# Four edits to a hybrid attention / state-space trunk step: a rotary table loaded earlier, softmax denominators of two heads inverted together, sample loads taken in turn, and a longer modelled pause

## The chip, the cores and the metric

The kernel runs on one core of one Trainium2 chip. The metric is the device time of one execution in microseconds (us). The engines are called as the profile calls them: PE (TensorE), DVE (VectorE), ACT (ScalarE), POOL (GpSimd), SP (SyncE, which here only issues DMAs). L383 is line 383 of the kernel.

## The reference

Two layers of a trunk in which three head groups work side by side on the same normalised input: latent attention, a matrix memory (mLSTM) and a gated delta rule. A layer, cut to what the change touches:

```python
proj = rms_norm(x, norm_w) @ w_in          # c_q, c_kv, k_r, z_a, ... z_m, z_g
q = (rms_norm(c_q, q_norm) @ w_uq).reshape(B, L, 8, 64 + 32)
q_nope, q_rope = q[..., :64], apply_rope(q[..., 64:], pos)
c_new = rms_norm(c_kv, kv_norm)            # latent of 256
o_a = mla_attention(q_nope, q_rope, c_all, kr_all, w_uk, w_uv, ...)
...
mixed = concat([o_a * silu(z_a), o_m * silu(z_m), o_g * silu(z_g)])
return x + mixed @ w_out, c_new, kr_new, ...
```

One new stream of 1024 frames and 16 meta tokens (the prompt) and 8 running streams of 16 frames (the samples) are stepped together: 1168 columns in all. The prompt's attention builds keys and values per head, with a chunk-causal mask. A sample attends, in latent space, over 1040 cached latents and its own 16 frames, so 8 batches of cache are read from HBM in each layer.

## The kernel before

Activations lie with features on the 128 rows (partitions) and the 1168 columns along the free side, in three slices (400, 384 and 384 columns). Wide tiles are "pages": a pool of 28, taken by `pg()` and given back by `free`; `room(n)` says whether n are free, `need(n)` waits for that. A value in float32 is multiplied as a high and a low part: `split` (L436 to L441) casts the high part on ACT and subtracts for the low part on DVE or POOL in turn, and `mm3` makes three matmuls of them.

The program is written by a weaver. Threads (`prep`, `att`, `samp_load`, `samp_ln`, ...) are Python generators; what one yields is a modelled number of microseconds to pause, or the name of an event to wait for. In the pauses the weaver writes the next piece of a filler: the projections, then `qkv` (queries, keys and values of the prompt), then the output projection. So the modelled pauses set the order in which instructions stand. On the chip each engine takes its own in that order, and waits on semaphores. `ld` (L382) issues loads on SP, whose loads and stores all stand in one queue; SP waits at the head of the queue for a buffer to come free.

**rstd** (L476) makes the column `1/sqrt(mean square)` and spreads it over 128 rows. PE sums squares with `onesb`, DVE scales (L495), POOL takes the power (L496), DVE splits it (L499, L500) and writes it into diagonal matrices (L506, L508). After a pause of 2.70 PE multiplies those by `onesr`. With `b16` it sums from a bfloat16 pair; that form is called six times in a layer, from `prep`, for the latent and the query part.

**prep** (L1343) normalises and splits the latents ckv (2 tiles) and cq (3 tiles), with two new pages for each tile. **qkv** waits until it is done and 10 pages are free, takes two for the rotary tables `tabq` and loads them, and computes query tiles; the first reads cq alone, the next reads the tables at L1420 and L1423.

**att** (L1568) runs over 8 heads, and for a head over three column pieces (336, 384 and 320 wide). The value matrix carries a block of ones, so the accumulator `po` holds the numerators on 64 rows and the denominators on the other 64; even and odd heads have them the other way round. The finish of a piece is five lines, L1612 to L1617: reciprocal of 64 rows on DVE, product of `po` and the gate z on DVE, product with the reciprocal on POOL, store from the ACT queue. z was loaded by SP into the tile "Og" (2 buffers) when the piece began, 64 rows at a time.

**The samples.** `samp_prep` (L1627) makes latent queries; `samp_load` (L1667) takes, for each batch, two pages of transposed latents (latT) and one of rotary keys (krT); `samp_ln` (L1709) takes latents in natural order (latN) with their last 32 rows from `latE` and `tok`; `samp_split` splits; `samp_s` computes scores and exponentials (L1753); `samp_t` transposes the weights and multiplies them by latN. Their first batches are woven into the last heads of `att`.

Of the kernel before, what the change touches and what calls it, by code (L numbers as in the profile page):

```python
# [19 lines left out]
T = 1168  # L20
# [287 lines left out]
def _build(nc, tc, ctx, I, O, layers):  # L308
# [29 lines left out]
    def room(n):  # L338
        return len(pages) + n <= NPG
# [136 lines left out]
    def rstd(out, a, dim, s0, s1, b16=False):  # L476
        w = s1 - s0
        tl = [c for c in range(NT) if s0 <= OFF[c] < s1]
        ps = pb()
        col = wt("col", 8)  # L480
        V.memset(col, 1.0)
        if b16:
            ab = wt("th", 800, 2, BF16)
            ah, al = ab[:, :w], ab[:, 400:400 + w]
            S.copy(ah, a)
            V.tensor_sub(al, a, ah)
        for j, c in enumerate(tl):
            n, o = LEN[c], OFF[c] - s0
            if b16:
                mm(ps[:n, j:j + 1], ah[:, o:o + n], onesb, True, False)  # L490
                mm(ps[:n, j:j + 1], al[:, o:o + n], onesb, False, True)
            else:
                mm(ps[:n, j:j + 1], a[:, o:o + n], ones[:, 0:1], True, True)
        for j0, j1, n in (((0, 1, 16), (1, len(tl), 128)) if tl[0] == 0 else ((0, len(tl), 128),)):
            V.tensor_scalar(col[:n, j0:j1], ps[:n, j0:j1], 1.0 / dim, EPS, op0=ALU.mult, op1=ALU.add)  # L495
        G.tensor_tensor(col[:, 0:len(tl)], col[:, 0:len(tl)], negh(len(tl)), op=ALU.pow)  # L496
        nt = len(tl)
        ch = wt("ch", 8, 2, F32R)
        V.tensor_copy(ch[:, 0:nt], col[:, 0:nt])  # L499
        V.tensor_sub(col[:, 0:nt], col[:, 0:nt], ch[:, 0:nt].bitcast(F32))  # L500
        dg = wt("dg", 1024, 1, F32R)
        first = 16 if tl[0] == 0 else 0
        for e, c_ in enumerate((ch, col)):
            o = 512 * e
            if first:
                V.tensor_scalar_mul(dg[:, o:o + 16], ident[:, 0:16], c_.bitcast(F32)[:, 0:1])  # L506
            m = nt - (first > 0)
            V.tensor_tensor(dg[:, o + first:o + w].rearrange("p (j t) -> p j t", t=128),  # L508
                            ident.unsqueeze(1).to_broadcast([128, m, 128]),
                            c_.bitcast(F32)[:, nt - m:nt].unsqueeze(2).to_broadcast([128, m, 128]), op=ALU.mult)  # L510
        yield 2.70
        ps = pb()
        for e in range(2):
            mm(ps[:, :w], onesr, dg[:, 512 * e:512 * e + w], e == 0, e == 1)
        if out is None:
            return ps[:, :w]
        S.copy(out, ps[:, :w])
# [69 lines left out]
    def layer(l, XH, XLp, XL, xres, xw, R):  # L587
# [755 lines left out]
        def prep():  # L1343
            yield ("cq", 2)
            yield from need(2)
            cq = [D1["cq", j] for j in range(3)]
            ckv = [D1["ckv", j] for j in range(2)]
            r1, r2 = pg(), pg()
            for s0, s1 in SLICES:
                w = s1 - s0  # L1350
                yield from rstd(r1[:, s0:s1], sumsq(ckv, w, s0, s1), 256.0, s0, s1, True)
                yield from rstd(r2[:, s0:s1], sumsq(cq, w, s0, s1), 384.0, s0, s1, True)
            while not room(4):
                yield 3.47
            yield 5.44
            hl = {}
            for n_, p_, r_, v_ in (("ck", ckv, r1, "kvn"), ("cq", cq, r2, "qn")):
                hl[n_] = []
                for k, t_ in enumerate(p_):
                    yield from need(2)  # L1360
                    hi, lo = pg(F32R), pg(F32R)
                    for s0, s1 in SLICES:
                        norm_split(t_, r_[:, s0:s1], vcol(l, v_, k), hi, lo, s0, s1)
                        yield 6.23
                    hl[n_].append((hi, lo))
                    if n_ == "cq":
                        free(t_)
                free(r_)
                if n_ == "ck":
                    for k in range(2):  # L1370
                        st(O["oLat"][l, k], ckv[k][:, :T])
                        G.tensor_copy(new[:, 128 * k:128 * k + 128], ckv[k][:, TP:T])
                    ps = pb()
                    for k in range(2):
                        tr(ps[:, 128 * k:128 * k + 128], ckv[k][:, TP:T], ident)
                    t_ = wt("hp", 528, 3)
                    S.copy(t_[:, 0:256], ps[:, 0:256])
                    st(tokS, t_[:, 0:256])
                    free(*ckv)
                A.update({n_ + "h": [x_[0] for x_ in hl[n_]], n_ + "l": [x_[1] for x_ in hl[n_]]})  # L1380
            D1["prep"] = 1

        KS = ((0, 348), (348, 694), (694, 1040))

        def qkv():
            while "prep" not in D1 or not room(10):
                yield "idle"
            tab, qs = [pg(), pg()], pg()
            A["qs"] = qs
            for j in range(2):  # L1390
                ld(tab[j][:, :T], I["tabq"][j])
            ckh, ckl, cqh, cql = A["ckh"], A["ckl"], A["cqh"], A["cql"]

            def load(t_):
# [172 lines left out]

        def att():  # L1568
            steps = [(h, s_, j) for h in range(8) for s_ in range(3) for j in range(9) if QB[j] < QS_[s_][1]]
            fly, po, zt = [], None, {}  # L1570
            for i_ in range(len(steps) + LA):
                if i_ < len(steps):
                    h, s_, j = steps[i_]
                    if s_ == j == 0:
                        while ("row", h) not in D1:
                            yield 0.3
                        yield max(0.0, D1["row", h] - W.t / 1000.0)
                    a, b = max(QS_[s_][0], QB[j]), QS_[s_][1]
                    if j == 0:
                        zt[h, s_] = z = wt("Og", 512)[64 * (h % 2):64 * (h % 2) + 64, :b - a]  # L1580
                        ld(z, mixS[8 + h // 2][64 * (h % 2):64 * (h % 2) + 64, a:b])
                    m = 80 if j == 0 else 128
                    qh, ql, kh, kl = A["sets"][h % 3]
                    ks = slice(KB[j], KB[j] + m)
                    ps = pb()[:m, :b - a]
                    mm(ps, kl[0:96, ks], qh[0:96, a:b], True, False)
                    mm(ps, kh[0:113, ks], qh[0:113, a:b], False, False)
                    mm(ps, kh[0:96, ks], ql[0:96, a:b], False, True)
                    pt = wt(("Tp", "M")[i_ % 2], 512)
                    S.activation(pt[:m, :b - a], ps, AF.Exp, scale=-1.0)  # L1590
                    fly.append((h, s_, j, a, b, m, pt))
                    if s_ == 2 and j == 8:
                        D1["hd", h] = 1
                        if h > 4:
                            free(*A["sets"][h % 3])
                if i_ >= LA:
                    h, s_, j, a, b, m, pt = fly.pop(0)
                    q0 = QS_[s_][0]
                    nj = sum(x_ < QS_[s_][1] for x_ in QB)
                    if j == 0:  # L1600
                        yield "v"
                        while A.get("fill", 0) and npa[0] - A["fill"] > 1:
                            yield 0.1
                        po = pa()
                        A["po"] = npa[0]
                    x_ = 4 * j + h // 2
                    v = VV_(x_ // 6)[:m, 192 * (x_ % 6) + 64 * (h % 2):192 * (x_ % 6) + 64 * (h % 2) + 128]
                    mm(po[:, a - q0:b - q0], v, pt[:m, :b - a], j == 0, j == nj - 1)
                    if j == nj - 1:
                        w = b - q0  # L1610
                        r, d = slice(64 * (h % 2), 64 * (h % 2) + 64), slice(64 - 64 * (h % 2), 128 - 64 * (h % 2))
                        rc, z = wt("hp", 528, 3)[r, :w], zt.pop((h, s_))  # L1612
                        V.reciprocal(rc, po[d, :w])  # L1613
                        V.tensor_mul(z, po[r, :w], z)
                        G.tensor_mul(z, rc, z)
                        A["po"] = 0
                        S.dma_start(mixS[8 + h // 2][r, q0:b], z)  # L1617
                yield YX
            free(*A["VV"])
            D1["att"] = 1  # L1620
# [46 lines left out]
        def samp_load():  # L1667
            yield "sprep"
            fly = A["fly"] = []
            for b in range(8):  # L1670
                for k in range(3):
                    while len(fly) >= RP or not room(1 + SR):
                        yield 0.30
                    raw = pg()
                    fly.append(raw)
# [316 lines left out]
```

## Time and profile before

| what | before |
| --- | --- |
| median of 3 runs | 2650.75 us (2647.45 to 2651.11) |
| the profiled execution | 2646.51 us, of which the span of the trace is 2644.6 |
| PE busy | 2488.7 us, 94% of the span |
| DVE, ACT, POOL busy | 58%, 42%, 29% |
| mean DMA rate | 98 GB/s |
| mean granted clock of PE | 0.978 of full |

The profiled execution lies a little under all three timed runs. PE is idle for some 156 us of the span; the rest of its time is work, apart from stretches in which the granted clock is half. "Waits" are idle time of an engine, put down to the instruction whose end released it.

### The profile page before, as it was taken

The page shows a single profiled execution, that of the slowest core. Times are in us where ns is not written, and L with a number is a line of the kernel's source. Part 1 is how long each engine was busy: PE and PEld are TensorE (multiplying, and loading weights), DVE is VectorE, ACT ScalarE, POOL GpSimd, SP SyncE. Part 2 cuts the span into 40 slices and gives each one's busy share as a digit, 9 for nine tenths or more (in the row PEclk, how much of TensorE's full clock was granted, in tenths as well). Part 3 has the DMA queues.
Part 4 walks back from the last instruction along what each step waited for, and adds up shares of the span by engine and source line. Part 5 has one row for each costly group of instructions (what it writes and reads, how often), then busy time and mean ns, then how long its engine had stood idle before and what let it go on. Part 6 is the DMA issues. An engine that isn't in the chain of part 4 may idle for free. (4 is left out here: it accounts for less than half of the span.)

```text
span 2644.6 us, 45521 instructions
## 1 busy us (share of the span) xinstructions
PE 2488.7 (94%) x17310; PEld 2150.1 (81%) x17310; DVE 1530.2 (58%) x3716; ACT 1116.4 (42%) x2635; POOL 764.6 (29%) x865
## 2 busy tenths in 40 slices
PE   6999999999999899979998999999999999999997
PEld 4887888878878789779977888788788788897896
DVE  6667475464453476654566774755743526665636
ACT  5363444444433433442343544444444434334612
POOL 3122222122123543232441222221221245332414
PEclk9999999999999999989998999999999999998998
DMA  3212112121123644464422121221211245444832
GB/s 130 73 39 70 51 53 83 51 69 51 59 71 126 179 119 123 126 219 163 141 76 51 43 75 52 62 73 51 69 52 58 85 157 149 113 121 147 286 117 80
DMA packets 158411, 258.67 MB, mean 98 GB/s; under 512 B 48704, under 2 KB 110768, under 8 KB 158192
## 3 DMA queue, kind: packets, MB, share of 16 engines
q1 hardware_dynamic: 152224, 247.59, 30.0%
q0 software_dynamic: 1856, 3.86, 0.7%
q10 hardware_dynamic: 4112, 4.30, 0.7%
q8 instruction: 137, 2.24, 0.3%
q14 instruction: 82, 0.67, 0.1%
HBM read 190.77 MB, written 64.92 MB: 97 GB/s over the span
## 5 line engine op out<-in xcount | busy, mean ns | idle before, releaser
L361 PE MATMUL pa<-pg,wh 128*128 128x384 f32 (+3 forms) x6324 | 1317.8, 351 | 17.7 <-DVE pg L441 7.0
L361 PEld LDWEIGHTS pa<-pg,wh 128*128 128x128 f32 x6324 | 1104.6, 190 | 59.9 <-issue 8.5
L361 PE MATMUL pb<-pg,pg 128*128 128x352 f32 (+26 forms) x1908 | 425.1, 338 | 18.3 <-DVE sm L1553 4.4
L361 PE MATMUL pa<-pg,wb 128*128 128x384 bf16 (+1 forms) x2208 | 420.3, 330 | 4.7 <-POOL pg L544 3.6
L361 PEld LDWEIGHTS pb<-pg,pg 128*128 128x128 f32 (+7 forms) x1908 | 301.1, 188 | 70.8 <-issue 14.0
L361 PEld LDWEIGHTS <-wb 128*128 128x128 bf16 x2208 | 201.6, 98 | 141.6 <-issue 28.9
L361 PE MATMUL pb<-wk,pg 128*128 128x128 f32 (+4 forms) x2168 | 223.1, 250 | 20.2 <-ACT wk L983 5.2
L441 POOL TENSOR_TENSOR wh<-wf,wh 128x1024 fp32r<-128x1024 f32 (+1 forms) x61 | 144.4, 2367 | 323.1 <-ACT wh L437 316.7
L361 PEld LDWEIGHTS pb<-wk,pg 128*128 128x128 f32 (+3 forms) x2168 | 194.2, 161 | 41.9 <-issue 16.7
L1590 ACT ACTIVATE wk<-pb 128x320 f32<-128x320 f32 (+8 forms) x288 | 114.1, 407 | 241.9 <-PE pb L361 222.5
L361 PE MATMUL pa<-wk,pg 128*128 128x320 f32 (+8 forms) x576 | 190.9, 417 | 1.9 <-ACT wk L1590 1.3
L437 ACT CAST wh<-wf 128x1024 fp32r<-128x1024 f32 (+1 forms) x122 | 126.4, 1036 | 129.8 <-PE pa L361 119.5
L1553 DVE TENSOR_REDUCE sm<-pb 128x1 f32<-128x348 f32 (+9 forms) x232 | 107.9, 493 | 102.4 <-PE pb L361 89.9
L1613 DVE RECIPROCAL wk<-pa 64x320 f32<-64x320 f32 (+2 forms) x48 | 110.7, 2305 | 48.2 <-PE pa L361 47.5
L361 PE MATMUL pb<-wk,wk 32*32 32x16 f32 (+6 forms) x1776 | 110.6, 216 | 13.7 <-DVE wk L1131 4.5
L1531 POOL TENSOR_TENSOR pg<-pg,pg 64x520 fp32r<-64x520 f32 (+1 forms) x64 | 86.9, 1369 | 111.0 <-ACT pg L1530 87.9
L868 DVE SCALAR_TENSOR_TENSOR pg<-pg,vec,pg 128x1192 f32<-128x1192 f32 x72 | 107.1, 1503 | 18.4 <-ACT pg L866 18.1
L441 DVE TENSOR_TENSOR wh<-wf,wh 128x1024 fp32r<-128x1024 f32 (+1 forms) x61 | 78.6, 1289 | 53.5 <-ACT wh L437 53.4
L693 ACT COPY pg<-pa 128x384 f32<-128x384 f32 (+1 forms) x108 | 52.1, 482 | 134.6 <-PE pa L361 133.4
L457 ACT CAST wb<-wf 128x1024 bf16<-128x1024 f32 x92 | 96.2, 1045 | 26.6 <-PE pa L361 20.1
L361 PEld LDWEIGHTS pa<-wk,pg 128*128 128x128 f32 (+1 forms) x576 | 97.9, 193 | 5.9 <-ACT wk L1590 1.9
L361 PEld LDWEIGHTS pb<-wk,wk 32*32 32x32 f32 (+2 forms) x1776 | 73.1, 122 | 32.3 <-issue 9.3
(298 smaller groups left out, 3205.7 us busy)
## 6 DMA issues: line engine op xcount, KB each, us to landing
wf<-win SPq DMA_DIRECT2D x92, 512.0 KB
pg<-latT SPq DMA_DIRECT2D x32, 520.0 KB
pg<-latN SPq DMA_DIRECT2D x32, 512.0 KB
wf<-wout SPq DMA_DIRECT2D x24, 512.0 KB
xa<-wk SPq DMA_DIRECT2D x40, 192.0 KB
mix<-pg SPq DMA_DIRECT2D x12, 584.0 KB
pg<-mix SPq DMA_DIRECT2D x12, 584.0 KB
mix<-pg SPq DMA_DIRECT2D x12, 576.0 KB
```

Source lines behind the costliest of these rows:

```text
L361: W.last = P.matmul(out, lhsT, rhs, start=start, stop=stop)
L437: S.copy(hi, src)
L441: lo_eng.tensor_sub(lo, src, hi.bitcast(F32))
L457: S.copy(wb[:, :n], wf)
L693: S.copy(o[:, s0:s1], ps)
L868: V.scalar_tensor_tensor(y[:, :n], cb[:, j:j + n], vcol(l, "cw", 4 * ti + j), y[:, :n], op0=ALU.mult, op1=ALU.add)
L1531: G.tensor_sub(lo, raw, hi.bitcast(F32))
L1553: V.tensor_reduce(mx[:LEN[c], 3 * c + i_:3 * c + i_ + 1], ps[:LEN[c], :n1 - x_], axis=AX.X, op=ALU.min)
L1590: S.activation(pt[:m, :b - a], ps, AF.Exp, scale=-1.0)
L1613: V.reciprocal(rc, po[d, :w])
```

## The change

1. `rstd` yields 4.00 instead of 2.70 for its `b16` calls.
2. `prep` takes the two table pages and loads them right after the latents' pages are freed, before cq is split; `qkv` waits for 8 free pages instead of 10.
3. `att` loads z once for a pair of heads, 128 rows, into tiles that alternate between the tags "Og" and "H". At each head's end ACT copies the denominators into their half of a 128-row tile, and DVE multiplies numerators by z. Only at the odd head one reciprocal runs over 128 rows, POOL multiplies, and one store of 128 rows follows: 24 loads, 24 reciprocals, 24 POOL products and 24 stores in each layer become 12 of each, and 24 copies on ACT are added.
4. `samp_load` loads batch b only after latN of batch b-1 has been issued.

```diff
-        yield 2.70
+        yield 4.00 if b16 else 2.70
...
                     free(*ckv)
+                    A["tab"] = [pg(), pg()]
+                    for j in range(2):
+                        ld(A["tab"][j][:, :T], I["tabq"][j])
...
         def qkv():
-            while "prep" not in D1 or not room(10):
+            while "prep" not in D1 or not room(8):
                 yield "idle"
-            tab, qs = [pg(), pg()], pg()
+            tab, qs = A["tab"], pg()
             A["qs"] = qs
-            for j in range(2):
-                ld(tab[j][:, :T], I["tabq"][j])
...
-                    if j == 0:
-                        zt[h, s_] = z = wt("Og", 512)[64 * (h % 2):64 * (h % 2) + 64, :b - a]
-                        ld(z, mixS[8 + h // 2][64 * (h % 2):64 * (h % 2) + 64, a:b])
+                    if j == 0 and h % 2 == 0:
+                        zt[s_] = z = wt(("Og", "H")[(3 * h // 2 + s_) % 2], (512, 516)[(3 * h // 2 + s_) % 2])[:, :b - a]
+                        ld(z, mixS[8 + h // 2][:, a:b])
...
-                        rc, z = wt("hp", 528, 3)[r, :w], zt.pop((h, s_))
-                        V.reciprocal(rc, po[d, :w])
-                        V.tensor_mul(z, po[r, :w], z)
-                        G.tensor_mul(z, rc, z)
+                        if h % 2 == 0:
+                            dt_[s_] = wt("hp", 528, 3)[:, :w]
+                        rc, z = dt_[s_], zt[s_]
+                        S.copy(rc[r], po[d, :w])
+                        V.tensor_mul(z[r], po[r, :w], z[r])
+                        if h % 2:
+                            V.reciprocal(rc, rc)
+                            G.tensor_mul(z, rc, z)
+                            S.dma_start(mixS[8 + h // 2][:, q0:b], z)
                         A["po"] = 0
-                        S.dma_start(mixS[8 + h // 2][r, q0:b], z)
...
-                    while len(fly) >= RP or not room(1 + SR):
+                    while len(fly) >= RP or not room(1 + SR) or b and ("ln", b - 1) not in D1:
                         yield 0.30
```

On ACT, before the first query tile of layer 0, the kernel before has these rows (L462 are the silus of the gate projections, L437 with `wh` a weight's high part, L1427 the end of the query tile's slices); the casts of cq stand further up, ahead of the silus shown:

```order
L462 ACTIVATE wk_8862<-pa_8833 128x400
L462 ACTIVATE wk_8892<-pa_8866 128x384
L437 CAST wh_9071<-wf_9070 128x768
L462 ACTIVATE wk_8925<-pa_8896 128x384
L1377 COPY wk_8956<-pb_8953 128x256
L462 ACTIVATE wk_8971<-pa_8930 128x400
L462 ACTIVATE wk_9001<-pa_8975 128x384
L462 ACTIVATE wk_9034<-pa_9005 128x384
L437 CAST wh_9076<-wf_9075 128x1024
L1427 ACTIVATE pg_9080<-pa_9081 128x400
L1427 ACTIVATE pg_9080<-pa_9092 128x384
L1427 ACTIVATE pg_9080<-pa_9103 128x384
```

After the change (lines move on by one) the same place reads:

```order
L462 ACTIVATE wk_9016<-pa_8990 128x384
L1377 COPY wk_9028<-pb_9025 128x256
L437 CAST wh_9076<-wf_9075 128x1024
L437 CAST pg_9035<-pg_7950 128x400
L437 CAST pg_9035<-pg_7950 128x384 x2
L437 CAST pg_9047<-pg_8068 128x400
L437 CAST pg_9047<-pg_8068 128x384 x2
L437 CAST pg_9058<-pg_8157 128x400
L437 CAST pg_9058<-pg_8157 128x384 x2
L1428 ACTIVATE pg_9080<-pa_9081 128x400
L1428 ACTIVATE pg_9080<-pa_9092 128x384
L1428 ACTIVATE pg_9080<-pa_9103 128x384
```

The nine casts of cq, three tiles of three slices, now stand behind the last silu and directly ahead of the query tile. Their low parts moved with them. On POOL the end of the same stretch was

```order
L441 TENSOR_TENSOR wh_9071<-wf_9070,wh_9071 128x768
L681 TENSOR_TENSOR pg_5936<-pg_5936,wk_8924 128x384
L681 TENSOR_TENSOR pg_6875<-pg_6875,wk_8970 128x400
L681 TENSOR_TENSOR pg_6875<-pg_6875,wk_9000 128x384
L681 TENSOR_TENSOR pg_6875<-pg_6875,wk_9033 128x384
```

and is now

```order
L681 TENSOR_TENSOR pg_6875<-pg_6875,wk_8985 128x384
L681 TENSOR_TENSOR pg_6875<-pg_6875,wk_9015 128x384
L441 TENSOR_TENSOR pg_9036<-pg_7950,pg_9035 128x384
L441 TENSOR_TENSOR pg_9048<-pg_8068,pg_9047 128x400
L441 TENSOR_TENSOR pg_9048<-pg_8068,pg_9047 128x384
L441 TENSOR_TENSOR pg_9059<-pg_8157,pg_9058 128x384
```

where four low parts of cq (`pg` from `pg`) stand behind the last gate product (L681); the other five stand likewise on DVE.

On SP, where the attention of layer 0 ends, the queue before goes (`mix` is read for z and for nothing else in these rows):

```order
L383 DMA pg_11702<-krT 96x1040
L383 DMA pg_11718<-latT 128x1040
L383 DMA pg_11721<-latT 128x1040
L383 DMA wk_11730<-mix 64x336
L383 DMA wk_11769<-mix 64x384
L383 DMA pg_11820<-krT 96x1040
L383 DMA pg_11823<-latT 128x1040
L383 DMA pg_11826<-latT 128x1040
L383 DMA wk_11869<-mix 64x320
L383 DMA pg_11940<-krT 96x1040
L383 DMA pg_11943<-latT 128x1040
L383 DMA pg_11974<-latT 128x1040
```

After the change:

```order
L383 DMA wk_11542<-mix 128x320
L383 DMA pg_11656<-latT 128x1040
L383 DMA pg_11659<-latT 128x1040
L383 DMA pg_11662<-krT 96x1040
L383 DMA pg_11762<-latE 16x128
L383 DMA pg_11762<-tok 16x128
L383 DMA pg_11763<-latE 16x128
L383 DMA pg_11763<-tok 16x128
L383 DMA pg_11762<-latN 128x1024
L383 DMA pg_11763<-latN 128x1024
L383 DMA pg_11772<-latT 128x1040
L383 DMA pg_11775<-latT 128x1040
```

The last z load now stands ahead of the first sample tile, and latN of batch 0 follows directly on its latT and krT; before, latN came after the latT of six batches.

On PE, between the sums and the broadcast of the second `rstd` call of layer 0, the rows are now (the sums are `onesb`, the broadcast is `onesr`):

```order
L361 MATMUL pb_8327<-onesb,wk_8330 128x1
L361 MATMUL pa_8311<-pg_122,wh_8159 128x384
L361 MATMUL pa_8311<-pg_123,wh_8159 128x384 x2
L361 MATMUL pa_8376<-pg_116,wh_8159 128x384 x2
L361 MATMUL pa_8376<-pg_117,wh_8159 128x384 x2
L361 MATMUL pa_8376<-pg_118,wh_8159 128x384 x2
L361 MATMUL pb_8383<-wk_8347,onesr 128x400
L361 MATMUL pa_8376<-pg_119,wh_8159 128x384 x2
L361 MATMUL pb_8383<-wk_8347,onesr 128x400
```

Nine projection matmuls stand between the last sum and the broadcast. Before, that call had 18 there, and the rows of the fourth call were

```order
L361 MATMUL pb_8424<-onesb,wk_8427 128x1
L361 MATMUL pa_8503<-pg_116,wh_8277 128x400
L361 MATMUL pa_8503<-pg_117,wh_8277 128x400 x2
L361 MATMUL pa_8503<-pg_118,wh_8277 128x400 x2
L361 MATMUL pa_8503<-pg_119,wh_8277 128x400 x2
L361 MATMUL pa_8503<-pg_120,wh_8277 128x400 x2
L361 MATMUL pa_8503<-pg_121,wh_8277 128x400
L361 MATMUL pb_8466<-wk_8441,onesr 128x384
```

which is ten; after the change the fourth call has eleven.

## Rows read from the trace of the kernel before

**Rows 1.** Windows: busy time by engine, PE clock, DMA share, GB/s; attention of layer 0, then its end
```profile
core 0: us, PE busy (x) PEld busy (x) DVE busy (x) ACT busy (x) POOL busy (x), PEclk, DMA share, GB/s
940.00:1080.00 140.00, 139.36 (x778) 125.44 (x777) 90.53 (x136) 47.78 (x113) 42.98 (x48) 1.00 0.41 113
1080.00:1220.00 140.00, 119.71 (x732) 105.44 (x731) 83.57 (x131) 69.19 (x183) 50.44 (x71) 0.91 0.61 201
```

**Rows 2.** The page's groups: the reciprocal
```profile
L1613 DVE RECIPROCAL wk<-pa 64x320 f32<-64x320 f32 (+2 forms) x48 | 110.7, 2305 | 48.2 <-PE pa L361 47.5
```

**Rows 3.** PE's waits by releaser, rstd stretch of layer 0, then of layer 1
```profile
PE pb L361 <- DVE wk L508: 5.1, 6, 2.3
...
PE pb L361 <- DVE wk L508: 4.2, 5, 1.5
```

**Rows 4.** Timeline of PE in the rstd stretch of layer 0
```profile
783.84 0.41 PE L361 MATMUL pb<-wk,onesr 128*128 128x384 f32 x1 [2.32 <-DVE wk L508]
```

**Rows 5.** Timeline of DVE, then of POOL, in the same stretch
```profile
753.22 2.34 DVE L499 CAST wk<-wk 128x4 fp32r<-128x4 f32 x1 [1.13 <-POOL wk L496]
...
752.16 1.02 POOL L496 TENSOR_TENSOR wk<-wk,neg 128x4 f32<-128x4 f32 x1 [21.89 <-DVE wk L495]
753.15 2.39 POOL L441 TENSOR_TENSOR wh<-wf,wh 128x1024 fp32r<-128x1024 f32 x1
```

**Rows 6.** Timeline of ACT, DVE and POOL: query and latent splits, layer 0
```profile
805.98 3.85 ACT L437 CAST pg<-pg 128x400 fp32r<-128x400 f32 x9
...
806.60 4.95 DVE L441 TENSOR_TENSOR pg<-pg,pg 128x400 fp32r<-128x400 f32 x5
...
807.40 6.52 POOL L441 TENSOR_TENSOR pg<-pg,pg 128x384 fp32r<-128x384 f32 x5 [22.29 <-ACT pg L437]
```

**Rows 7.** Timeline of ACT, DVE and POOL where the query tiles begin
```profile
839.42 1.04 ACT L437 CAST wh<-wf 128x1024 fp32r<-128x1024 f32 x1
...
843.80 0.49 ACT L1427 ACTIVATE pg<-pa 128x384 f32<-128x384 f32 x1 [1.08 <-PE pa L361]
...
840.50 1.86 DVE L441 TENSOR_TENSOR wh<-wf,wh 128x1024 fp32r<-128x1024 f32 x1 [0.32 <-ACT wh L437]
...
840.26 1.01 POOL L681 TENSOR_TENSOR pg<-pg,wk 128x384 f32<-128x384 f32 x1 [3.09 <-DVE wk L463]
```

**Rows 8.** Timeline of PE there
```profile
850.04 8.21 PE L361 MATMUL pa<-pg,wh 128*128 128x346 f32 x50 [0.50 <-DVE wk L1423]
```

**Rows 9.** PE's waits by releaser, 1130 to 1172, and one row of its timeline there
```profile
PE pa L372 <- ACT pg L1753: 7.2, 3, 4.1
...
PE pa L372 <- DVE wk L1614: 2.2, 1, 2.2
...
1146.44 6.93 PE L361 MATMUL pb<-wk,pg 128*128 128x128 f32 x36 [4.09 <-DMA pg<-latN]
```

**Rows 10.** Timeline of SP: sample loads behind gate loads, layer 0
```profile
1104.19 10.89 SPq L383 DMA_DIRECT2D wk<-mix  x2
...
1142.14 0.89 SPq L383 DMA_DIRECT2D pg<-latN  x2
```

**Rows 11.** Timeline of DVE, then of PE, layer 1, where the splits stand behind a reciprocal
```profile
2399.76 2.56 DVE L1613 RECIPROCAL wk<-pa 64x384 f32<-64x384 f32 x1 [6.44 <-PE pa L361]
...
2404.73 6.78 PE L361 MATMUL pb<-pg,pg 96*128 96x320 f32 x21 [2.55 <-DVE pg L441]
...
2442.24 2.42 PE L361 MATMUL pb<-pg,pg 128*128 128x352 f32 x7 [2.35 <-ACT pg L1753]
```

**Rows 12.** Timeline of PE in the steady run of sample batches, layer 1
```profile
2464.41 4.18 PE L361 MATMUL pb<-wk,pg 128*128 128x128 f32 x36
...
2473.16 4.18 PE L361 MATMUL pb<-wk,pg 128*128 128x128 f32 x36
```

**Rows 13.** Windows of the steady run
```profile
2450.00:2490.00 40.00, 39.72 (x307) 38.32 (x306) 28.69 (x48) 25.80 (x66) 15.64 (x27) 1.00 0.85 272
```

**Rows 14.** Groups of ACT in 2440 to 2500: casts of the sample tiles
```profile
L1698 ACT CAST pg<-pg 128x528 fp32r<-128x528 f32 x24 | 14.0, 640 | 2.1 <-DMA pg<-latT 2.1
```

More of the change, by code (lines that the diff above doesn't have):

```diff
@@ L1569, in att @@
             steps = [(h, s_, j) for h in range(8) for s_ in range(3) for j in range(9) if QB[j] < QS_[s_][1]]
-            fly, po, zt = [], None, {}
+            fly, po, zt, dt_ = [], None, {}, {}
             for i_ in range(len(steps) + LA):
```

## The prediction

> **What bounds the kernel now.** The table of busy shares comes first: PE works 94% of the span, so time can only come from the idle 6% of PE, or from stretches in which its clock is half. The windows show where these lie [rows 1]. In the attention of layer 0 PE is busy 139.4 of 140 us at clock 1.00: what DVE saves there is worth nothing. In the next 140 us it is busy 119.7 us at 0.91: that stretch, in which the samples begin, has some 20 us to give, and a little for its clock. So I read every edit by the wait at PE that it moves, with three questions: which wait, how long, what stands ahead of it now.
>
> **Part 1, the longer pause in rstd.** PE waits for L508, the diagonal matrices, 5.1 us in layer 0 and 4.2 us in layer 1 [rows 3]; the longest wait is 2.32 us, at the last call [rows 4]. I counted, for each of the six calls of layer 0, the projection matmuls that stand between the last sum and the broadcast. Before, they are 18, 18, 13, 10, 13 and 13; now 27, 9, 16, 11, 20 and 14. The longer pause pushes the sums of the next call apart as well, so the second call loses half its cover. A matmul of 384 columns takes 0.17 us (50 in 8.21 us, a little shorter ones, stand in [rows 8]). The first call gains 9 x 0.17 = 1.5 us, the third and the fifth 0.5 and 1.2, the second loses 1.5, the others stay. At the first call one part of the chain is DVE's cast L499, 2.34 us for 4 columns, which ended when POOL's split that started just before it ended (753.15 + 2.39 = 755.54; 753.22 + 2.34 = 755.56) [rows 5]; on POOL that split still follows the power. Gains count only up to the waits that were there, the loss in full, and the last call, which waited longest, has one matmul more, 0.17 us: I take -1 us for both layers. Bounds: -6 (the spreading does not matter) and +3 (the second call waits 1.5 us in each layer and nothing is gained).
>
> The Trainium skill, page "SBUF — State Buffer", section "Who interferes with whom", says that a DVE instruction in a two-port mode, or with two SBUF inputs, and a GpSimd instruction that reads SBUF take one shared port pair in turn, the later one blocked for the whole instruction. The pair of rows just named agrees with it.
>
> **Part 2, the table sooner.** What it removes: PE waited 0.50 us for L1423, which had waited for the table [rows 8]. Twice, that is -1 us. What it adds is found in the order: the two pages are taken before cq is split, each cq tile needs two more, and the nine casts now stand behind the last silu. Before, nine such casts (the last latent tile and two of cq) took 3.85 us on ACT from 805.98, and ten low parts ran beside and behind them until 813.9 on DVE (4.95 us for five) and POOL (6.52 for five) [rows 6], 25 us before the first query tile. Now they begin after the cast of the weight, 839.42 + 1.04 = 840.46 [rows 7]. The nine casts end 3.85 us later, at 844.3. POOL's four low parts begin after its last gate product, 840.26 + 1.01 = 841.27, and take 4 x 1.30 = 5.2 us: 846.5. DVE's five begin after the weight's low part, 840.50 + 1.86 = 842.36, and take 4.95 us: 847.3. PE takes the tile's matmuls in order, so the tile ends about 1 us after the last low part, at 848.3; before, its last slice was evicted at 843.80. The delay is 4.5 us a layer, and nothing covers it: the projections, which would be the filler, are over. PE then works in drops for about 8 us, and half-clock matmuls may follow (27 matmuls x 0.17 = 4.6 us more if the whole tile is at half clock). I take 4.5 + 1 in each layer, +11. Bounds: +7 (the earlier slices overlap better than I laid them out) and +20 (all at half clock).
>
> By the page's rule the low parts on DVE and POOL exclude each other, since both read two SBUF tiles; the last part would then be done after 4 x 1.01 + 5 x 0.70 = 7.5 us from 841.27 (an estimate: a POOL product of that size took 1.01, and DVE's 1.86 for 1024 columns make 0.70 for 384 [rows 7]), at 848.8 instead of 847.3. The sum would be 3 us higher over both layers.
>
> **Part 3, the pair of heads.** 48 reciprocals take 110.7 us of DVE [rows 2]; half go. They lie in the full stretch, so this saves nothing by itself. What counts is the end. In layer 1 the query splits of `samp_prep` stood behind a reciprocal of 2.56 us; PE then waited 2.55 us and worked at half clock, 21 matmuls in 6.78 us [rows 11], so half of that, 3.4, was lost too. Head 6 is even and has no reciprocal now, so this place should shrink. I count -5 for layer 1 (0 to -10: another wait, 2.35 us for the exponentials at 2442.24, may stay, go or grow). In the other attention pieces the accumulator is released sooner: the reciprocal of 2.2 us no longer stands ahead of the product. I take -2. The 48 copies on ACT cost some 0.4 us each; they stand ahead of exponentials that PE waits for, but ACT is busy 47.8 of 140 us [rows 1]: 0, at most +5.
>
> **Part 4, z loads and sample loads on SP.** Two rows carry this. SP stood 10.89 us at two z loads, held by the store of the tile's previous use, and latN of batch 0 was issued only at 1142.14 [rows 10]. PE ran dry: it waited 4.09 us for latN, 7.2 us in three waits for the exponentials and 2.2 us for the last product of the attention [rows 9], 13.5 us, and then 36 matmuls took 6.93 us [rows 9] where they take 4.18 in the steady run [rows 12], 2.75 us of half clock. Now latN of batch 0 stands directly behind krT of batch 0 and z loads no longer stand between. The scores of batches 0 and 1 and the products of batch 0 lie inside the last head. The exponentials' waits remain in part: layer 1, whose batches 0 and 1 came earlier, still paid 2.35 us for one [rows 11]. So -13.5 - 2.75 + 3.25 = -13. Bounds: -18 (all goes, and 2 us of half clock besides) and -4 (latN alone is cured).
>
> **Sum** against the profiled execution, 2646.51 us: -1 - 1 + 11 - 5 - 2 - 13 = -11, so 2635.5. The median of the runs shown lies 4.2 us above the profiled one; on its scale I predict 2650.75 - 11 = 2640 us.
>
> **Rivals.** *More is won* (2626): the low parts arrive in the order in which PE needs them, so that Part 2 costs +7, and the samples give -18 and -8. For it: the first query tile needs cq one tile at a time. Against it: PE works in order and has nothing else. -1 - 1 + 7 - 8 - 2 - 18 = -23, rounded to 2627. *No net change* (2654): the run-dry only moves. The last head must now share DVE, ACT and POOL with the splits of two batches, so the exponentials are late again at its end; Part 4 gives -5, layer 1 nothing: -1 - 1 + 11 - 2 - 5 = +2, 2653. For it: 7.2 of the 13.5 us are waits for exponentials, not for a load. *Slower* (2661): loads taken in turn come too late in the steady run. There a batch takes 8.75 us on PE [rows 12], PE is full (39.7 of 40 us) and the DMA engines are busy 0.85 at 272 GB/s [rows 13]. latT and krT of a batch are 2 x 520 + 390 KB, 5.4 us at that rate, behind latN's 1024 KB, 3.9 us; then the last casts, some 2 of 0.64 us [rows 14], and a low part: about 11 us from issue to use. In the new order SP may issue them about 11 to 13 us before PE needs them. ACT already stood 2.1 us for latT [rows 14]. If each of some six steady batches in two layers waits 1.8 us, that is +22, so +11 in all. It decides from about 0.9 us a batch. *The pause and the table undo each other and nothing else is felt* is within the second.
>
> **How the numbers follow.** The forecast (-4 to -18 us) has 0.38, more won 0.16, no net change 0.22, the loads in turn 0.16, Part 2 at its upper bound with a weak Part 4 0.08. A measurement of this kernel tells about 0.2%, 5.3 us, from no change. Faster: 0.38 + 0.16 = 0.54; same 0.22; slower 0.24. The range reaches from 2620 (bounds -6 + 7 - 1 - 10 - 2 - 18 = -30) to 2661 (the loads in turn); the forecast alone has 2633 to 2647.
>
> **What the profile after would show.** Part 1: fewer waits for L508 at the first and last calls, one new of over 1 us at the second. Part 2: a wait at PE of 4 to 6 us in all for L437 or L441 just ahead of the first query tile, in both layers, and no wait for the table. Part 3: the reciprocals at 24, and no wait of 2.55 us for L441 at 2404. Part 4: SP's waits for the stores of z gone, no wait for latN, less than 5 us for L1753 in layer 0. I am wrong if the query tile starts without a wait (then the casts were not late), if PE waits in every steady batch for sample tiles, or if the exponentials at the end of the attention wait as long as before.

## The result and the profile after

The change made the kernel slower: 2687.48 us (2685.84 to 2689.03, 4 runs) against 2649.10 us (2647.41 to 2651.11, 4 runs), a ratio of 1.0144, 95% interval 1.0127 to 1.0162. That is +38 us, where -11 was forecast and the range ended at 2661. PE's waits by releaser, over the whole span of the kernel after (us in total, times, longest), begin with the row of L508, which fell (20.0 before). The other rows shown are ones that the kernel before did not have or had smaller:

```profile
PE pb L361 <- DVE wk L508: 16.9, 13, 4.7
PE pa L361 <- DVE pg L441: 11.2, 8, 1.8
...
PE pb L361 <- ACT pg L1703: 9.4, 9, 1.2
PE pb L361 <- POOL pg L1704: 8.8, 12, 1.2
...
PE pb L361 <- DVE pg L1704: 6.0, 7, 1.3
...
PE pb L361 <- DMA pg<-wukT: 4.6, 1, 4.6
PE pa L361 <- ACT pg L437: 4.0, 2, 2.0
PE pb L361 <- DVE pg L1707: 3.9, 5, 1.3
```

The four rows of L1703, L1704 and L1707 are casts and low parts of the sample tiles: 28.1 us, against 1.4 on the same lines before. The L437 row is new, and the L441 row rose from 7.0. Two large rows of the kernel before are gone, the waits for latN and for the sample exponentials (L1753):

```profile
PE pa L372 <- ACT pg L1753: 7.9, 4, 4.1
...
PE pb L361 <- DMA pg<-latN: 4.1, 1, 4.1
```

The waits can be placed by windows (columns as in [rows 1]). In the kernel after, for the query tiles, the attention of layer 0, and its end with the samples:

```profile
840.00:880.00 40.00, 31.49 (x149) 28.04 (x150) 14.82 (x21) 15.91 (x35) 20.00 (x23) 0.87 0.57 172
960.00:1080.00 120.00, 120.00 (x672) 108.81 (x671) 67.10 (x110) 48.34 (x111) 33.06 (x37) 1.00 0.40 116
1080.00:1240.00 160.00, 136.18 (x746) 114.73 (x745) 78.38 (x136) 74.26 (x195) 46.20 (x69) 0.89 0.55 182
```

The first and the last of these windows in the kernel before:

```profile
840.00:880.00 40.00, 35.90 (x185) 32.50 (x184) 12.61 (x25) 15.61 (x35) 20.07 (x27) 0.96 0.71 207
1080.00:1240.00 160.00, 139.71 (x860) 125.40 (x859) 89.72 (x143) 71.36 (x187) 50.44 (x71) 0.93 0.56 186
```

The attention is full, as before. Where the query tiles begin PE is idle for 8.5 of 40 us, against 4.1 before. In the sample stretch it is idle for 24 of 160 us, against 20 before, at a clock of 0.89 against 0.93; it also gets through fewer matmuls there, 746 against 860. At the query tiles the timeline shows the queues one after the other (PE, then ACT, DVE, POOL):

```profile
841.17 0.63 PE L361 MATMUL pa<-pg,wh 128*128 128x400 f32 x2 [1.99 <-ACT pg L437]
843.64 2.60 PE L361 MATMUL pa<-pg,wh 128*128 128x400 f32 x7 [1.84 <-DVE pg L441]
847.55 4.70 PE L361 MATMUL pa<-pg,wh 128*128 128x400 f32 x16 [1.32 <-DVE pg L441]
...
839.63 1.06 ACT L437 CAST wh<-wf 128x1024 fp32r<-128x1024 f32 x1
840.58 3.86 ACT L437 CAST pg<-pg 128x400 fp32r<-128x400 f32 x9
848.29 0.50 ACT L1428 ACTIVATE pg<-pa 128x400 f32<-128x400 f32 x1 [3.85 <-PE pa L361]
...
852.63 0.49 ACT L1428 ACTIVATE pg<-pa 128x384 f32<-128x384 f32 x1 [1.29 <-PE pa L361]
...
842.22 5.74 DVE L441 TENSOR_TENSOR pg<-pg,pg 128x400 fp32r<-128x400 f32 x5
...
841.61 5.46 POOL L441 TENSOR_TENSOR pg<-pg,pg 128x384 fp32r<-128x384 f32 x4 [0.39 <-ACT pg L437]
```

Nine casts start at 840.58, five low parts on DVE last until 847.96, and four on POOL until 847.07. PE waits three times, 5.15 us in all. The tile's first slice leaves at 848.29, 7.6 us later than before, and its third at 852.63, 8.8 us later than before (843.80 in [rows 7]). The first slice of the kernel before:

```profile
840.66 0.51 ACT L1427 ACTIVATE pg<-pa 128x400 f32<-128x400 f32 x1 [0.20 <-PE pa L361]
```

In the steady run of samples, which [rows 12] showed for layer 1 at one batch in 8.75 us, the timeline of the kernel after reads, in layer 0 (PE, ACT, SP):

```profile
1179.28 4.18 PE L361 MATMUL pb<-wk,pg 128*128 128x128 f32 x36
1184.67 2.27 PE L361 MATMUL pb<-pg,pg 128*128 128x352 f32 x9 [1.21 <-ACT pg L1703]
1187.23 0.58 PE L361 MATMUL pb<-pg,pg 128*128 128x352 f32 x2 [0.28 <-POOL pg L1704]
1188.98 0.62 PE L361 MATMUL pb<-pg,pg 128*128 128x352 f32 x1 [1.17 <-POOL pg L1704]
...
1193.74 3.73 PE L361 MATMUL pb<-wk,pg 128*128 128x128 f32 x32
...
1183.83 0.27 ACT L1801 COPY pg<-pb 128x128 f32<-128x128 f32 x1 [4.08 <-DVE pg L1801]
1183.99 2.23 ACT L1703 CAST pg<-pg 128x528 fp32r<-128x528 f32 x4
...
1177.60 1.23 SPq L383 DMA_DIRECT2D pg<-latT  x2
```

The products of a batch (matmuls of `wk` and `pg`) start at 1179.28, those of the next at about 1193: 14 us. The casts (L1703) start where the copy behind the products (L1801) ends, and PE then waits for them and for the low parts. The loads issued at 1177.60 come up again below. The saving on DVE itself came as written in the order, 110.7 us of reciprocals [rows 2] down to 55.3, with 21.1 us of copies added on ACT. It lies in the attention, where PE is full before and after, so it was worth nothing there:

```profile
L1619 DVE RECIPROCAL wk<-wk 128x320 f32<-128x320 f32 (+2 forms) x24 | 55.3, 2303 | 0.6
...
L1616 ACT COPY wk<-pa 64x320 f32<-64x320 f32 (+2 forms) x48 | 21.1, 440 | 6.9 <-PE pa L361 5.8
```

### The profile page after: what moved, and what is told of

The parts are those of the page before. It is cut to its first block, busy times and chain, and to the rows that moved or that the text cites. A ratio compares the mean times of both kernels' runs of the same rounds, so it can differ in the third digit from the quotient of the medians.

```text
span 2685.7 us, 45336 instructions
## 1 busy us (share of the span) xinstructions
PE 2512.5 (94%) x17310; PEld 2164.6 (81%) x17310; DVE 1475.2 (55%) x3692; ACT 1136.4 (42%) x2683; POOL 743.9 (28%) x841
## 5 line engine op out<-in xcount | busy, mean ns | idle before, releaser
L361 PE MATMUL pb<-pg,pg 128*128 128x352 f32 (+26 forms) x1908 | 444.7, 345 | 46.9 <-ACT pg L1703 9.4
L361 PEld LDWEIGHTS pb<-pg,pg 128*128 128x128 f32 (+7 forms) x1908 | 306.9, 192 | 107.0 <-POOL pg L1704 13.4
L441 POOL TENSOR_TENSOR wh<-wf,wh 128x1024 fp32r<-128x1024 f32 (+1 forms) x63 | 148.9, 2364 | 328.5 <-ACT wh L437 328.5
L361 PEld LDWEIGHTS pb<-wk,pg 128*128 128x128 f32 (+3 forms) x2168 | 192.4, 160 | 37.1 <-issue 16.4
L437 ACT CAST wh<-wf 128x1024 fp32r<-128x1024 f32 (+1 forms) x122 | 126.4, 1036 | 131.7 <-PE pa L361 121.1
L441 DVE TENSOR_TENSOR wh<-wf,wh 128x1024 fp32r<-128x1024 f32 (+1 forms) x59 | 75.2, 1275 | 73.7 <-ACT wh L437 73.5
L681 POOL TENSOR_TENSOR pg<-pg,wk 128x384 f32<-128x384 f32 (+1 forms) x48 | 49.1, 1024 | 185.2 <-DVE wk L463 175.7
```

Source lines behind the costliest of these rows:

```text
L361: W.last = P.matmul(out, lhsT, rhs, start=start, stop=stop)
L437: S.copy(hi, src)
L441: lo_eng.tensor_sub(lo, src, hi.bitcast(F32))
L681: G.tensor_mul(o[:, s0:s1], o[:, s0:s1], th[:, :s1 - s0])
```

## The experiments

Each kernel is compared with the kernel before on the same chip; times are medians, ratios stand with their 95% interval. Where a result gives no time for the kernel before, it is the one named last. "The gate" is the clause that edit 4 adds; where a run has edit 4 and something more, the diff shows only what is more.

**Each edit alone.** The four pieces of the diff, one at a time.

> Edit 1 alone. Theory A (the two traces: the last silu before the query tiles ended at the same time in both kernels): no change, -2 to +2 us. Rival: the longer pause moves later pieces of the weave and carries part of the loss, +5 us or more.

2644.30 against 2649.99, 0.9984 (0.9969 to 0.9999): some 4 us faster, if anything.

> Edit 2 alone. Theory A (the early pages push the splits of cq behind the projections; the first query tile ended 7.6 us later in each layer): +14 to +18 us, with waits of PE for L437 and L441 ahead of the first query tile. Rival: that delay is made up in the attention, whose start is not what sets its end, and this edit costs under 4 us.

2647.86, 0.9989 (0.9971 to 1.0006): no change. My theory missed: alone, the early pages cost nothing. They do move the nine casts of cq, from some 807 to 812 us in the kernel before to 832 to 837 (timeline of ACT), but that is still ahead of the last silu (L462), and the first query tile is no later than the stretch ahead of it.

```profile
832.07 3.03 ACT L437 CAST pg<-pg 128x400 fp32r<-128x400 f32 x7
...
839.90 0.49 ACT L462 ACTIVATE wk<-pa 128x384 f32<-128x384 f32 x1 [2.81 <-PE pa L361]
```

> Edit 3 alone. Theory A: it removes the waits of SP for the stores of z and the reciprocal ahead of the query splits, -5 to -15 us. Rival: moving the z loads moves the load of wukT or the first sample tiles too, and it costs 5 us or more.

2649.35, 0.9999 (0.9984 to 1.0014): no change, neither the gain nor the loss. Its trace shows a loss and a gain that cancel: the last sample exponential of layer 0 comes 8.6 us later than before, that of layer 1 at the same time. In layer 0 PE waits for the weight `wukT`, and behind that wait the granted clock is 0.50 from 1095 to 1115 us (timeline of PE, then windows):

```profile
1091.02 7.88 PE L361 MATMUL pb<-pg,pg 64*128 64x128 f32 x25 [3.06 <-DMA pg<-wukT]
...
1080.00:1120.00 40.00, 36.88 (x130) 27.39 (x128) 10.04 (x24) 14.25 (x42) 4.47 (x8) 0.66 0.40 113
```

SP issued `wukT` at 1084.57, 6.5 us ahead of its first use at 1091.02, behind the load of a weight of the output projection; before, it was issued at 1077.55, 12 us ahead of its first use at 1089.71. In the same stretch the waits for latN and for the exponentials are also longer than before (5.8 and 9.2 us against 4.1 and 7.2), and no run moves `wukT` alone, so its share of the 8.6 us is not shown.

> Edit 4 alone. Theory A (each batch's latT stands on SP behind latN of the batch before, which waits for POOL's memsets, which stand behind POOL's low parts of the batch before: a ring of some 14 us a batch where PE needs 8.75): +20 to +30 us, and a spacing of about 14 us between the products of two batches. Rival: the ring comes only with the paired loads, and this edit alone costs under 5 us.

2676.03, 1.0099 (1.0071 to 1.0127): +26 us. One edit of four carries most of the loss.

**Two and three edits.** The pieces together.

> Edits 1 and 2 together, each of which alone changed nothing that can be told. Theory B (the pause delays the splits of the latents by some 6 us, and only then the two early pages are missing when cq is to be split): +12 to +18 us, with the nine casts of cq behind the last silu, and 7 us or more until the first query tile. Rival (the loss of 16 us needs the paired heads, whose tiles or copies hold ACT): within 4 us of before.

2665.04 against 2649.22, 1.0066 (1.0042 to 1.0089): +16 us, from two edits that alone gave -4 and -2 (the -2 within the noise). The casts now stand behind the last silu, and PE at the first query tile has the waits of the kernel after (timeline of ACT, then of PE):

```profile
836.76 0.49 ACT L462 ACTIVATE wk<-pa 128x384 f32<-128x384 f32 x1 [3.62 <-PE pa L361]
838.35 3.86 ACT L437 CAST pg<-pg 128x400 fp32r<-128x400 f32 x9
...
838.94 0.63 PE L361 MATMUL pa<-pg,wh 128*128 128x400 f32 x2 [1.99 <-ACT pg L437]
841.41 2.69 PE L361 MATMUL pa<-pg,wh 128*128 128x400 f32 x7 [1.84 <-DVE pg L441]
845.28 14.95 PE L361 MATMUL pa<-pg,wh 128*128 128x400 f32 x73 [1.18 <-DVE pg L441]
```

> Edits 1 and 2, but the two table pages are taken and loaded at the end of prep, when cq has been split. Theory B (pages): the delay of the query tile is gone, within 4 us of before. Rival (the pause alone puts the splits late once the table is out of the way of qkv): +12 us or more, as with edits 1 and 2.

```diff
-                    A["tab"] = [pg(), pg()]            # behind free(*ckv)
-                    for j in range(2): ld(...)
...
+            yield from need(2)                         # behind the last split of cq
+            A["tab"] = [pg(), pg()]
+            for j in range(2): ld(A["tab"][j][:, :T], I["tabq"][j])
             D1["prep"] = 1
```

2643.82, 0.9977 (0.9965 to 0.9989): the loss is gone, and something of a gain is left. The casts stand where they stood in the kernel before, and the query tile has no wait (timeline of ACT, then of PE):

```profile
805.70 3.85 ACT L437 CAST pg<-pg 128x400 fp32r<-128x400 f32 x9
...
838.46 10.96 PE L361 MATMUL pa<-pg,wh 128*128 128x400 f32 x60
```

So it is the pages: the two that the tables take early are ones that cq needs, and its casts wait until others come free. With edit 2 alone they come some 25 us later than before, just ahead of the last silu; with the longer pause as well they come another 6 us later (832.07 to 838.35), behind it. The pause alone leaves them where they were (806.37).

> The change without edit 4. Theory A (the gate costs some 26 us by itself, wherever the z loads stand): 2687 - 26 = 2661 us, and no waits of PE for the sample tiles' casts and low parts in the steady batches. Rival (paired z loads and the gate share their cost): 2672 us or more.

2669.55, 1.0075 (1.0058 to 1.0092): +20 us, between the two expectations. Taking the gate out gives 18 us, less than its 26 alone.

> The change without edit 2. Theory B (pause and early table cost 16 us together): 2687 - 16 = 2671 us, the first query tile within 1 us of the kernel before. Rival: 2680 us or more, because the sample stretch of each layer makes its own time.

2664.53, 1.0057 (1.0040 to 1.0073): +15 us. Taking the table out gives 23 us, more than the 16 of pause and table and more than either expectation; the parts do not add exactly.

**What the gate does.** The theory so far (A in the expectations) was a ring through SP's queue: latT of the next batch behind latN, which waits for POOL's memsets, which stand behind POOL's low parts. Its rival (C) was that the casts merely stand in a bad place on ACT.

> Edit 4 alone, and latE and tok are issued from POOL's queue instead of SP's, so that SP no longer waits for POOL's memsets ahead of latN and the next latT. Theory A (the ring goes through SP's wait for the memsets, which stand behind POOL's low parts): most of the 26 us is won back, 2655 us or less, casts of a batch no longer directly after the copy behind the products. Rival C (what delays the scores is that the casts stand on ACT behind that copy, whenever the loads come): 2670 us or more, with latT landed before the casts begin.

```diff
-   ld(te[96:112], I["latE"]...)
-   ld(te[112:128], tokS[...])
+   ld(te[96:112], I["latE"]..., G)     # issued from POOL's queue
+   ld(te[112:128], tokS[...], G)
```

2645.68 against 2647.49, 0.9990 (0.9977 to 1.0002): all 26 us back.

> The kernel before with latE and tok issued from POOL's queue, as a measure of that edit by itself. Both theories: within 5 us of before, since the steady batches of before had PE full.

2647.47, 1.0002 (0.9987 to 1.0017): the edit by itself changes nothing.

> Edit 4 alone, loosened by one batch: batch b waits for latN of batch b-2. Theory A: SP is a batch ahead, so the ring has 2 x 8.75 us for its 14: within 5 us of before. Rival C (the place of the casts on ACT follows the gate all the same): 10 us or more.

```diff
-   or b and ("ln", b - 1) not in D1
+   or b > 1 and ("ln", b - 2) not in D1
```

2648.14, 0.9999 (0.9988 to 1.0011): a gate that looks one batch further back costs nothing.

All three came out as the ring has it. The traces do not fit it. In the trace of edit 4 alone, layer 1, SP and ACT show:

```profile
2481.66 0.83 SPq L383 DMA_DIRECT2D pg<-latT  x2
...
2499.84 0.27 ACT L1796 COPY pg<-pb 128x128 f32<-128x128 f32 x1 [4.62 <-DVE pg L1796]
2500.00 2.23 ACT L1698 CAST pg<-pg 128x528 fp32r<-128x528 f32 x4
```

In each layer ACT casts the batches in the order in which SP loads them; counted off, the tiles issued at 2481.66 (the sixth of eight batches) are those cast at 2500.00, 18 us later. In the kernel after it is the same: the tiles issued at 1177.60, the sixth batch of layer 0, are cast at 1198.00. The DMA engines were nearly idle from 2488 to 2494 (windows, the last two columns are DMA share and GB/s):

```profile
2482.00:2488.00 6.00, 4.89 (x42) 4.68 (x40) 1.37 (x4) 1.58 (x5) 0.00 (x0) 1.00 1.00 340
2488.00:2494.00 6.00, 4.40 (x24) 3.27 (x24) 3.04 (x5) 4.32 (x12) 3.81 (x7) 1.00 0.19 50
```

so these tiles had landed when ACT came to them. It came late because in its order they stood behind the copy of the products (L1796). That makes a ring too, out of orders alone: casts, low parts, scores, then the products on PE, the copy, the next casts. With latE on POOL's queue the order is another one: the casts follow the last copy of transposed weights (L1784), ahead of the copy of the products, so they run beside the products, and the batch takes 8.7 us:

```profile
2475.48 0.27 ACT L1796 COPY pg<-pb 128x128 f32<-128x128 f32 x1 [2.48 <-DVE pg L1796]
...
2479.28 0.27 ACT L1784 COPY wk<-pa 128x128 f32<-128x128 f32 x1 [0.17 <-PE pa L372]
2479.44 2.23 ACT L1698 CAST pg<-pg 128x528 fp32r<-128x528 f32 x4
2484.15 0.27 ACT L1796 COPY pg<-pb 128x128 f32<-128x128 f32 x1 [2.48 <-DVE pg L1796]
```

So that run had changed two things. So had the gate that looks further back: in its trace two of a batch's four casts stand at 2484.78 and two at 2487.25, all ahead of the copy of the products at 2491.93, as in the kernel before. Two more kernels change the order and leave SP's queue as the gate has it.

> Edit 4 alone, with both halves of the copy behind a batch's products (L1796) on DVE, so that on ACT the casts of a sample tile no longer stand behind one. SP's queue is as in edit 4 alone. Theory C (order: the tiles had been loaded 18 us before their casts, which stood behind that copy): 5 us or more of the 26 come back; not all, since the low parts on DVE still stand behind the copies there. Theory A (the ring through SP): 2670 us or more, as edit 4 alone.

```diff
-   (S.copy if r else V.tensor_copy)(A["OL"][r]..., po...)
+   V.tensor_copy(A["OL"][r]..., po...)
```

2655.39 against 2647.09, 1.0027 (1.0014 to 1.0040): +8 us instead of +26. The casts follow L1784 directly (2482.72 and 2482.88); the low parts on DVE still stand behind the copies there (2477.79 behind 2477.38).

> The same, with all low parts of latT on POOL too, so that neither casts nor low parts stand behind the copies. POOL's memsets, and so SP's waits, come later than in edit 4 alone. Theory C: 2660 us or less. Theory A: 2676 us or more, because the ring through POOL and SP gets longer by two low parts a batch.

```diff
-   (G if k else V).tensor_sub(lo[:, sl], raw[:, sl], ...)
+   G.tensor_sub(lo[:, sl], raw[:, sl], ...)
```

2648.65, 1.0004 (0.9990 to 1.0018): nothing is left of the 26 us, with twice as many low parts on POOL ahead of the memsets that SP waits for. The ring through SP falls; the order on ACT and DVE is the cause. (The two kernels also differ a little in where the weaver put other rows.)

**The whole change, mended.**

> The whole change, with latE and tok on POOL's queue. If the costs are those of the parts: the gate's 15 to 25 us come back, the 17 us of pause and table stay: 2662 to 2672 us.

2659.82, 1.0048 (1.0029 to 1.0068): +13 us, a little under the expectation. What is left is near the 16 us of pause and table.

> The whole change with both mended: table pages taken after cq is split, latE and tok on POOL's queue. If the costs are those of the parts, nothing is left of the 38 us: 2640 to 2650 us, and faster than before if the paired z loads then give back the waits at the end of the attention.

2638.56, 0.9965 (0.9951 to 0.9979): 8.5 us faster than before, a little more than expected, and the best version here. It has all four edits, with the pages of the tables taken after cq is split, and latE and tok on POOL's queue. The first query tile runs without a wait; the wait for `wukT` in layer 0 is still there:

```profile
841.46 11.18 PE L361 MATMUL pa<-pg,wh 128*128 128x400 f32 x60
...
1094.24 6.04 PE L361 MATMUL pb<-pg,pg 64*128 64x128 f32 x25 [3.00 <-DMA pg<-wukT]
```

> Edits 1 and 3, with the tables loaded early but their pages taken after cq is split. If the costs add: -6 us (tables and pause) and 0 (pair), 2643 us. If the pause moves the paired loads to a worse place, as the change without edit 2 or 4 leaves open: 2650 us or more.

2644.63 against 2647.49, 0.9995 (0.9979 to 1.0012), without the gate: between the two expectations, nearer the first. The kernel above has the gate and the other queue besides, and 0.9965; the two intervals just touch, so that the two help together once the casts stand well is likely and not settled.

## Why the prediction was wrong

**The step that failed** is Part 4 and the weight of the rivals. I took -13 us for latN coming sooner, put the steady batches at nothing in the sum, and set their cost aside as the rival *the loads in turn*, at 0.16 and +22 us. With edit 4 alone the kernel is 26 us slower. The loss is that rival's in place and size, but not in its mechanism. I had priced bytes and issue times, 11 us from issue to use against 11 to 13; the loads had 18 us and were in time. What I did not read from the order, although it was there, was where the casts stand on ACT relative to the copy of the products. The waits for latN (4.1 us) and for the exponentials (7.9 and 2.3) did vanish, as said; the new waits for casts and low parts, 28.1 us, are more than they were. My second sign of being wrong, that PE waits in every steady batch for sample tiles, is what came.

**The range** was one-sided. At its lower end, 2620, all parts stand at their best bounds together; at its upper end, 2661, only the loads in turn stand against the forecast, with every part at its forecast. With the upper bounds that I had written myself (+3, +20, +5 for the copies, Part 4 at -4, Part 3 at 0) the parts sum to +21 with the other terms (-1 and -2) as they are, 2672 us, and with the rival's +22 to 2694, which the measured time lies within. (Two rivals' headings are also a little off their sums: 2626 where the sum gives 2628, and 2654 where it gives 2653.)

**Part 2** had the right mechanism at the right place: casts and low parts of cq late, waits for L437 and L441, no wait for the table. PE's waits there, 5.15 us in layer 0 and 5.05 in layer 1, are within the 4 to 6 that I named. The low parts ended at 847.96 and 847.07 where I had 847.3 and 846.5. The term was +11. From the last silu of the projections (L462) to the last copy of the keys (L1459, now L1460) the kernel after takes 8.7 us longer in layer 0 and 7.9 in layer 1, 16.6 together, and the kernel with edits 1 and 2 is 16 us slower. So the term was 5 us too small, inside its bounds of +7 to +20. I had the tile's end 1 us behind the last low part. It came 4.7 us behind it, at 852.63, because some 16 of the tile's matmuls still stood behind the last wait and took 4.70 us; the granted clock from 845 to 850 us was 0.50. I put the term on edit 2; it needs edit 1 as well.

By the rule of the Trainium skill, page "SBUF — State Buffer", section "Who interferes with whom", I had the last low part 1.5 us later, at 848.8; it ended at 847.96, between the rule's 848.8 and the 847.3 from the rows. Each of the five took 1.15 us on average beside POOL's; those of [rows 6], which also ran beside POOL's for most of their time, took 0.99.

**Part 1**: the wait for L508 in layer 0 went from 5.1 to 3.8 us, with one of 0.82 at the second call, where I had foreseen over 1. That is near the -1 forecast; alone the edit may be worth 4.

**Part 3**: the full attention hid the saving on DVE, as said. Some 5 us did come in layer 1: with edit 3 alone the kernel is 4.8 us late at the first exponential of its attention and 0.1 at the last of its samples. What I missed is a cost in layer 0, 8.6 us at its last sample exponential: there the load of `wukT` moved behind other work on SP, PE waited 3.06 us for it, and its matmuls then ran at a granted clock of 0.50. I had not listed what stands behind the z loads on SP.

**What stays open.** The single effects (-4, -2, 0 and +26) sum to 20; pause and table together cost 16 instead of -6, 22 more, which makes 42 where 38 was measured. Leaving out one edit gave 18 for the gate and 23 for the table, so the parts are not independent. For the pair and the gate the traces show more, each from one execution. From the last copy of the keys to the last sample exponential the kernel before takes 345.7 us in layer 0 and 337.2 in layer 1. The pair alone adds 8.2 and -6.8, the gate alone 7.8 and 17.3, and the whole change 16.5 and 9.9: in this stretch the two add up, to within 1 us in each layer. With the gate alone 9 of these 25 us are idle time of PE and 16 are longer busy time for the same matmuls, at about the same mean clock (0.95 and 0.95 before, 0.95 and 0.94 with the gate); how the 16 arise was not taken apart.

## What to carry to other kernels

When a load is gated, look for what else the gate moves: the place of its consumers in an engine's order is fixed when the program is written, and a load that lands in time is worth nothing if its cast stands behind the copy of an earlier result. Two edits that are each free can be slow together when they use the same reserve, here two pages and six microseconds. Test an edit's parts alone and in pairs before mending one of them, and look at both queues that a mend changes before reading a cause from its time.

## What the runs showed of the hardware that I had not expected

In the kernel with edit 3 alone the granted clock was 0.66 over 1080 to 1120 us, a mean of its two levels: it was 1.00 until 1090, 0.60 from 1090 to 1095, where a wait of PE of 3.06 us for `wukT` ended, and 0.50 from 1095 to 1115, though PE then showed no further wait. PE was busy 36.9 of the 40 us. Before, PE was busy 37.1 us in the same stretch, and the clock stayed at 1.00, with waits of 1.28 us at most.
